# A feed-forward block on one core: a third Winograd pair, its products summed in two PSUM banks, and copies moved to ScalarE

## The chip, the cores and the metric

The kernel runs on one core of a Trainium2 chip. Four engines matter: TensorE (PE in the profile) multiplies, reading its operands from SBUF and adding its results up in PSUM, which has eight banks of 128 x 512 numbers; VectorE (DVE) and ScalarE (ACT) do elementwise work; GpSimd (POOL) does a little. Loads are issued from SyncE's queue (SP). Each engine works through its own queue in order and waits there for semaphores of the others. The metric is the device time of one execution in microseconds (us), smaller is better.

## The reference, cut to what matters

One block of a streaming encoder on 256 tokens of width 1024, in float32: a half-weighted feed-forward, a mixer of two branches (a gated linear recurrence, "HGRN", and a forgetting attention), a cross attention to a memory of 256 rows, and a second half-weighted feed-forward. Every stage has an RMS norm before and after.

```python
def swiglu(h, w_in, w_down):
    gate, up = jnp.split(h @ w_in, 2, axis=-1)
    return (jax.nn.silu(gate) * up) @ w_down

h = rmsnorm(x, ffn1_pre_g[l])
x = x + 0.5 * rmsnorm(swiglu(h, ffn1_w_in[l], ffn1_w_down[l]), ffn1_post_g[l])
...  # mixer, cross attention
h = rmsnorm(x, ffn2_pre_g[l])
x = x + 0.5 * rmsnorm(swiglu(h, ffn2_w_in[l], ffn2_w_down[l]), ffn2_post_g[l])
```

`w_in` is 1024 x 5632 and `w_down` 2816 x 1024 in each feed-forward.

## The kernel before

**Numbers in two parts.** Each float32 operand x is split in a rounded part `hi` (a cast, by ScalarE) and a remainder `lo` = x − hi (a subtraction, by VectorE). A product is then three matmuls, hi·hi + hi·lo + lo·hi. `load_split` does this for a weight tile of 128 x 1024 that SyncE has loaded into a `raw` buffer (lines 147 and 149), `split` for any other tile (lines 167 and 168). Buffers rotate: 4 `raw`, 8 `hi`, 8 `lo`, and 4 `extra` in which the tiles `sraw` of weights to be summed lie. A load waits until the tile that was in its buffer has been split or summed.

**Chunks of a feed-forward.** `ffn` works through 11 chunks (`NFF`) of 256 gate and 256 up columns of `w_in`; a chunk's weights are four tiles of 128 x 1024. There are four ways to make a chunk:

- *by tokens* (`act_tok`): for each half h of 128 tokens, 24 matmuls of 512 columns (gate and up beside each other) into one `mm` bank. `act_evac` then makes silu(gate) on ScalarE and its product with up on VectorE, and `flush` turns the result into columns with four transposes (line 438) into a `tr` bank, which is split.
- *by columns* (`act_col`): the weights are the stationary operand and the result is already transposed. Four blocks, each of 8 matmuls of 512 columns (weights' hi with both parts of x beside each other, class `Joined`), and 8 of 256 (weights' lo with the tokens' hi). `added` adds the two halves of the bank: a copy `plo` on ScalarE (line 219) and an addition on VectorE (line 221), four times a chunk.
- *first* (`act_first`): the chunks at the beginning, block by block of the inner dimension as the data arrive. Chunks 0, 1 and 2 of the first feed-forward are made so; the second makes its chunks 0 and 1 by tokens.
- *as a pair* (`act_pair(c, between)`): chunks c and c + 1 together, by Winograd's form of the 2 x 2 block product with seven block products instead of eight. The blocks of the left operand are two halves of the tokens by two halves of the inner dimension, those of the right operand two halves of the inner dimension by two chunks. Each of the seven `product`s is 12 matmuls of 512 columns. The left sums are made once in a feed-forward by `pair_inputs` (tiles `ss` and `sx`); it starts from `xf`, the input in float32, which in the first feed-forward `pair_joined` adds up out of hi and lo on VectorE (line 512). The right sums are made for each pair on VectorE (`add`, line 578), eight additions of 128 x 1024, on tiles that `sum_load` and `raws` have loaded. Seven products take 14 splits of 128 x 1024. The product p1 is needed twice, so it is copied out of its bank (`S.copy(p1, b0)`), as is p3; v, w and the outputs `c11`, `c01`, `c10` are combined by five VectorE operations of 128 x 512.

`PAIRS` and `TOKS` say how the later chunks are made; what is in neither is made by columns:

```python
TOKS = {"f1_in": (), "f2_in": (2, 5)}
PAIRS = {"f1_in": (6, 9), "f2_in": (3, 6, 9)}
```

So in the first feed-forward chunks 3, 4, 5 and 8 are made by columns, and (6, 7) and (9, 10) are pairs; in the second only chunk 8 is made by columns.

**Down projections.** `down(c, h)` multiplies a chunk's activations by two tiles of `w_down`, into four `acc` banks that add up all chunks. The kernel puts them between the chunks and, inside a pair, between the products: `between` is a list of halves of down projections and `step_between` issues the next one (12 matmuls of 512 columns). The last three chunks' down projections come at the end.

**PSUM.** 4 `acc` banks, 2 `mm`, 2 `tr`. A pair uses an `mm` bank for p1 and, added to it, the product with the raw block (b0); three `tr` allocations for b2, b3 and b1; and a second `mm` bank for b4, in which the products ad and e are added up one after the other.

**What sets the order.** The program's order is that of the code, moved by a scheduler that takes dependencies and priorities: work under `tc.high_priority()` goes ahead on its engine, `tc.issue_after(x)` holds it back until x, and `after(i)` places work behind the i-th matmul (`log`). On TensorE matmuls stand as they are issued; `flush(n)` places the transposes of a chunk 21 or so matmuls into later work. On VectorE and ScalarE splits, sums, combinations and evacuations are interleaved in the order in which the scheduler takes them to become ready.

**Start.** Eight `head` tiles hold a block of x (transposed), its gains and 512 columns of weights. For each, ScalarE casts the weights (line 785) and the gained x (`gain_split`, line 366; the first one's hi is made by VectorE), and VectorE makes both remainders.

**The HGRN stage.** The recurrence's score products are made in six sets (`SETS`), each at `after(r0 + R_AT[si])`, between the matmuls of the gates (`proj_tok` with 344 columns, line 1044) and of the attention's k and q. Between sets `grow` multiplies decays into K and Q on VectorE (lines 973 to 996), `gather` and `stash` copy parts out of them on ScalarE, and `keep` takes the products out of PSUM. `grow` overwrites the K and Q that the set before has read. The gates' `mm` banks are evacuated by ScalarE (line 1046) and VectorE (line 1047).

## Time and profile before

| | |
|---|---|
| median of three runs | 774.85 us (774.65 to 775.62) |
| profiled execution | 773.87 us, span 771.6 us |
| granted TensorE clock | 0.998 |
| TensorE busy | 763.9 us (99%) |
| VectorE busy | 647.0 us (84%) |
| ScalarE busy | 493.5 us (64%) |
| first feed-forward | about 5 to 173 us of the span |
| HGRN products' first three sets | about 258 to 288 us |

The profile comes from one execution. Its span runs from the first to the last instruction; the time of the execution is 2.3 us longer. In a timeline row stand the start, the busy time, the engine, the line of the code, the operation, what is written and read (buffer numbers left out), the shape and the count; in brackets the idle time of that engine just before and what ended it. Nearly all matmuls have line 97, that of the helper `MM`, so they are told apart by the tiles that they write and read. Matmuls are pipelined: the duration of one is longer than the distance to the next. A group row gives the count, then the busy time in us and the mean in ns, then idle time before the group's instructions. In a row of a window stand the start and end, its length, the busy time and count of TensorE, of its weight loads, of VectorE, of ScalarE and of GpSimd, the granted clock, the share of DMA time and the GB/s.

### The profile page before, as it was taken

Reading aid. Unit: us, or ns where it says so; the run is one execution under the profiler, and the core shown is the slowest. Engines: PE = TensorE matmul, PEld = TensorE weight load, DVE = VectorE, ACT = ScalarE, POOL = GpSimd, SP = SyncE. Lnnn points to the kernel's source line nnn. Section 1 sums busy time; section 2 is a strip of 40 time slices with the busy share of each in tenths; the row PEclk is TensorE's granted clock in tenths of the full one; section 3 lists DMA queues with packets and bytes.
Section 4 is the critical chain, followed back from the end, with each engine's and each line's share of the span. In section 5 each row is a group of like instructions: output and inputs, shape, how many; then the busy total and the mean of one; then the engine's idle time right before and its main releaser. Section 6 shows DMA issues by size and latency. Waiting matters only on the chain.

```text
span 771.6 us, 11832 instructions
## 1 busy us (share of the span) xinstructions
PE 763.9 (99%) x4398; PEld 650.3 (84%) x4398; DVE 647.0 (84%) x992; ACT 493.5 (64%) x803; POOL 17.2 (2%) x39
## 2 busy tenths in 40 slices
PE   9999999999999999999999999999999999999996
PEld 7888888888888998898888888889888888888885
DVE  7798998998778899988776665885679999999993
ACT  7666565768764678667676345862768567665762
POOL 0000000000000101200000000000000000000000
PEclk9999999999999999999999999999999999999999
DMA  9758386255744445834576654456075726467231
GB/s 339 267 197 290 120 287 248 93 203 196 226 164 147 168 155 186 307 108 158 199 264 234 216 169 161 165 186 223 24 247 186 259 110 216 167 231 287 82 138 55
DMA packets 44505, 148.06 MB, mean 192 GB/s; under 512 B 5144, under 2 KB 8864, under 8 KB 44448
## 3 DMA queue, kind: packets, MB, share of 16 engines
q1 hardware_dynamic: 43168, 144.83, 53.5%
q0 software_dynamic: 848, 2.12, 1.0%
q8 instruction: 34, 0.56, 0.3%
q10 hardware_dynamic: 432, 0.37, 0.1%
q14 instruction: 23, 0.19, 0.1%
HBM read 146.24 MB, written 1.06 MB: 191 GB/s over the span
## 4 chain that ended last, share of the span: by engine, by line
PE 98%; DMA 1%; DVE 0%; ACT 0%; issue 0%; SPq 0%; DVEq 0%; ACTq 0%
PE mm L97 45%; PE acc L97 39%; PE tr L97 12%; PE tr L438 1%; PE tr L379 1%; DMA head<-in_head_dram 1%; PE tr L1211 0%; PE tr L1305 0%; PE acc L1424 0%; DVE xs L415 0%; DVE post L410 0%; ACT hi L785 0%; ACT hlT L366 0%; SPq L769 0%; SPq L764 0%
## 5 line engine op out<-in xcount | busy, mean ns | idle before, releaser
L149 DVE TENSOR_TENSOR lo<-raw,hi 128x1024 fp32r<-128x1024 f32 (+1 forms) x212 | 251.4, 1202 | 37.5 <-ACT hi L147 30.9
L147 ACT CAST hi<-raw 128x1024 fp32r<-128x1024 f32 (+1 forms) x212 | 215.4, 1034 | 74.4 <-PE mm L97 35.0
L97 PE MATMUL mm<-hi,hlT 128*128 128x512 f32 (+1 forms) x624 | 190.2, 381 | 0.0
L97 PEld LDWEIGHTS mm<-hi,hlT 128*128 128x128 f32 x624 | 115.3, 188 | 19.7
L97 PE MATMUL mm<-lo,hlT 128*128 128x512 f32 (+1 forms) x312 | 117.5, 381 | 0.0
L97 PE MATMUL acc<-hi,act 128*128 128x512 f32 x352 | 113.4, 390 | 0.0
L97 PEld LDWEIGHTS acc<-hi,act 128*128 128x128 f32 x352 | 66.1, 188 | 13.7 <-ACT act L167 0.3
L167 ACT CAST hi<-sraw 128x1024 fp32r<-128x1024 f32 x50 | 52.0, 1054 | 27.3 <-DVE sraw L578 19.4
L97 PE MATMUL acc<-lo,act 128*128 128x512 f32 x176 | 69.4, 394 | 0.0
L97 PEld LDWEIGHTS mm<-lo,hlT 128*128 128x128 f32 x312 | 58.5, 188 | 9.7 <-DVE lo L149 0.2
L97 PE MATMUL acc<-hlT,hi 128*128 128x512 f32 x256 | 64.4, 393 | 0.0
L168 DVE TENSOR_TENSOR lo<-sraw,hi 128x1024 fp32r<-128x1024 f32 x50 | 60.2, 1218 | 0.0
L97 PEld LDWEIGHTS acc<-hlT,hi 128*128 128x128 f32 x256 | 46.1, 189 | 8.3
L97 PE MATMUL mm<-hlT,hi 128*128 128x512 f32 (+1 forms) x192 | 44.0, 357 | 0.0
L97 PE MATMUL tr<-hi,sx 128*128 128x512 f32 x120 | 39.3, 391 | 0.0
L97 PEld LDWEIGHTS acc<-lo,act 128*128 128x128 f32 x176 | 33.1, 188 | 7.2 <-DVE lo L149 0.7
L97 PEld LDWEIGHTS acc<-hlT,lo 128*128 128x128 f32 x256 | 35.0, 190 | 2.5
L97 PEld LDWEIGHTS mm<-hlT,hi 128*128 128x128 f32 x192 | 33.2, 189 | 4.4
L97 PE MATMUL acc<-hlT,lo 128*128 128x256 f32 x256 | 36.2, 283 | 0.0
L578 DVE TENSOR_TENSOR sraw<-sraw,raw 128x1024 f32<-128x1024 f32 x30 | 35.9, 1219 | 0.1
L97 PE MATMUL tr<-hlT,hi 128*128 128x512 f32 x128 | 32.6, 394 | 0.0
L97 PE MATMUL mm<-hlT,lo 128*128 128x256 f32 x160 | 27.7, 284 | 0.0
(293 smaller groups left out, 1277.1 us busy)
## 6 DMA issues: line engine op xcount, KB each, us to landing
raw<-in_wts_dram SPq DMA_DIRECT2D x227, 512.0 KB, 4.3
sraw<-in_wts_dram SPq DMA_DIRECT2D x20, 512.0 KB, 5.1
raw<-in_gf_dram SPq DMA_DIRECT2D x12, 344.0 KB, 3.8
head<-in_head_dram SPq DMA_DIRECT2D x7, 392.0 KB, 6.6
grow<-in_rows_dram SPq DMA_DIRECT2D x4, 512.0 KB, 5.4
xs<-in_x_dram SPq DMA_DIRECT2D x2, 512.0 KB, 7.8
cbm<-cd POOLq DMA_DIRECT2D x2, 512.0 KB, 6.4
brow<-in_rows_dram SPq DMA_DIRECT2D x4, 256.0 KB, 3.6
```

The lines of the kernel that those rows point to most:

```text
L97: log.append(PE.matmul(*args, **kw).ins)
L147: S.copy(h, r)
L149: V.tensor_tensor(out=l, in0=r, in1=h.bitcast(F32), op=ALU.subtract)
L167: a = S.copy(hi, src)
L168: b = V.tensor_tensor(out=lo, in0=src, in1=hi.bitcast(F32), op=ALU.subtract)
L379: PE.transpose(blocks[-1][1], src(kb), ident)
L438: PE.transpose(trv[:, j, h * P : (h + 1) * P], ats[c, h][:, j * P : (j + 1) * P], ident)
L578: V.tensor_tensor(out=x, in0=x, in1=y, op=ALU.add)
```

## The change

Six things change together.

1. `PAIRS["f1_in"]` gets a third pair, (4, 5), which stands directly before the pair (6, 7). Those chunks were made by columns.
2. `TOKS` gets chunks 3 and 8 in the first feed-forward and chunk 8 in the second. Those were made by columns.
3. `act_pair` adds its products up in two `mm` banks: b1 holds p1, then + aed, + ad, + e; b4 holds de, then + baed. Signs of the left sums and the roles of the two chunks are turned round so that each partial sum is a wanted term: after p1, after aed (v) and after ad (w), ScalarE copies b1 out; after de it copies b4 (p5). The product with the raw block, b0, has a `tr` bank of its own. VectorE combines three times instead of five (`c01` = b4 − v, `c11` = p5 − w, `c00` = p1 + b0); the fourth output is read from b1 directly. ScalarE copies four times instead of two.
4. The products come in the order p1, de, aed, baed, ad, b0, e (before: p1, baed, de, aed, b0, ad, e), and the right sums are made in that order, still eight additions a pair.
5. `xf` of the first feed-forward is made in the start by ScalarE, eight activations of 128 x 256 straight from the heads, instead of four VectorE additions of 128 x 512 in chunk 2.
6. The first three entries of `R_AT` go from 24, 126, 210 to 66, 130, 188.

```diff
@@ -33,9 +33,9 @@
 
 STAG = 3
 
-TOKS = {"f1_in": (), "f2_in": (2, 5)}
-
-PAIRS = {"f1_in": (6, 9), "f2_in": (3, 6, 9)}
+TOKS = {"f1_in": (3, 8), "f2_in": (2, 5, 8)}
+PAIRS = {"f1_in": (4, 6, 9), "f2_in": (3, 6, 9)}
 
 L_ACT = 21
 L_F1 = 24
@@ -53,7 +53,7 @@
 M_T = (106, 119)
 M_O = (136, 140)
 
-R_AT = (24, 126, 210, 252, 286, 318)
+R_AT = (66, 130, 188, 252, 286, 318)
 
 R_GROW = ((1, 0), (2, 1))
 
@@ -505,6 +505,8 @@
 
 
 
         def pair_joined(k):
             t = m4([P, 4, T], n="xf")
             for i in range(2):
@@ -525,11 +527,11 @@
             ss = [m4([P, 2, 4, P], n="ss") for _ in range(2)]
             de, aed, ad, baed = (t[:, i] for t in ss for i in range(2))
             V.tensor_tensor(out=de, in0=d, in1=e, op=ALU.subtract)
-            V.tensor_tensor(out=aed, in0=a, in1=de, op=ALU.subtract)
+            V.tensor_tensor(out=aed, in0=de, in1=a, op=ALU.subtract)
             V.tensor_tensor(out=ad, in0=a, in1=d, op=ALU.subtract)
-            V.tensor_tensor(out=baed, in0=b, in1=aed, op=ALU.subtract)
+            V.tensor_tensor(out=baed, in0=b, in1=aed, op=ALU.add)
             out = {}
-            for n, x in (("baed", baed), ("aed", aed), ("de", de), ("ad", ad), ("e", e)):
+            for n, x in (("de", de), ("aed", aed), ("baed", baed), ("ad", ad), ("e", e)):
                 t = m4([P, 2, 4, P], F32R, "sx")
                 split(t[:, 0], t[:, 1], x)
                 out[n] = t
@@ -544,7 +546,7 @@
             return t
 
         def more(r, c, k, n, j, op):
-            src = wts[_AT[w_in] + 4 * (c + n) + 2 * k + j - 4]
+            src = wts[_AT[w_in] + 4 * (c + 1 - n) + 2 * k + j - 4]
             if op is None:
                 loads.append(nc.sync.dma_start(r, src).ins)
             else:
@@ -592,52 +594,48 @@
                 return sp.tile([P, 512], F32, tag="z2", name=nm(n), bufs=3)
 
             sums, both = sums_of_pair.pop(c)
-            vw = m4([P, 2, 512], n="vw")
-            pc = m4([P, 2, 512], n="pc")
-            p1, p3, v, w = pc[:, 0], pc[:, 1], vw[:, 0], vw[:, 1]
-            b0 = mm()
-            product(b0, of_x(0), splits(sums), True)
-            S.copy(p1, b0)
+            copies = [m4([P, 2, 512], n=n) for n in ("vw", "pc")]
+            p1, v, w, p5 = (t[:, i] for t in copies for i in range(2))
+            b1 = mm()
+            product(b1, of_x(0), splits(sums), True)
+            S.copy(p1, b1)
+            add(sums, both)
             for _ in range(2 if c == 3 else 1):
                 step_between()
-            b2 = trp()
+            b4 = mm()
+            product(b4, of("de"), splits(sums), True)
+            S.copy(p5, b4)
+            step_between()
             raw = raws(1, 1)
-            product(b2, of("baed"), splits(raw), True)
-            S.copy(p3, b2)
+            add(sums, raw)
+            product(b1, of("aed"), splits(sums), False)
+            S.copy(v, b1)
             step_between()
-            add(sums, both)
+            product(b4, of("baed"), splits(raw), False)
             add(both, raw)
-            b3 = trp()
-            product(b3, of("de"), splits(sums), True)
-            add(sums, raw)
-            step_between()
-            b1 = trp()
-            product(b1, of("aed"), splits(sums), True)
             with tc.high_priority():
-                V.tensor_tensor(out=v, in0=p1, in1=b1, op=ALU.subtract)
-                V.tensor_tensor(out=w, in0=b3, in1=v, op=ALU.subtract)
-            step_between()
-            raw = raws(1, 0)
-            product(b0, of_x(1), splits(raw), False)
-            with tc.high_priority():
-                act_evac(b0, c, 0)
-            add(sums, raw)
-            step_between()
-            b4 = mm()
-            product(b4, of("ad"), splits(both), True)
+                t = half_tile("c01")
+                V.tensor_tensor(out=t, in0=b4, in1=v, op=ALU.subtract)
+                act_evac(t, c, 0)
+            product(b1, of("ad"), splits(both), False)
+            S.copy(w, b1)
             with tc.high_priority():
                 t = half_tile("c11")
-                V.tensor_tensor(out=t, in0=w, in1=b4, op=ALU.subtract)
-                act_evac(t, c + 1, 1, r2[0], q)
-                t = half_tile("c01")
-                V.tensor_tensor(out=t, in0=w, in1=p3, op=ALU.add)
+                V.tensor_tensor(out=t, in0=p5, in1=w, op=ALU.subtract)
+                act_evac(t, c, 1, r2[0], q)
+            step_between()
+            b0 = trp()
+            raw = raws(1, 0)
+            product(b0, of_x(1), splits(raw), True)
+            add(sums, raw)
+            with tc.high_priority():
+                t = half_tile("c00")
+                V.tensor_tensor(out=t, in0=p1, in1=b0, op=ALU.add)
                 act_evac(t, c + 1, 0)
             step_between()
-            product(b4, of("e"), splits(sums), False)
+            product(b1, of("e"), splits(sums), False)
             with tc.high_priority():
-                t = half_tile("c10")
-                V.tensor_tensor(out=t, in0=v, in1=b4, op=ALU.add)
-                silu = act_evac(t, c, 1, r2[0], q)
+                silu = act_evac(b1, c + 1, 1, r2[0], q)
             if c + 1 == NFF - 1:
                 table(silu)
             while between:
@@ -721,7 +719,7 @@
                 accs = [[acc(), acc()], [acc(), acc()]]
             if c == 2 and pairs:
                 if first_half:
-                    xf = [pair_joined(k) for k in range(2)]
+                    xf = xf1
                 pairs_in = pair_inputs()
 
             while done < (NFF - STAG if last == NFF - 1 else min(c - 1 - (c + 1 in pairs), NFF - STAG - 1)):
@@ -755,6 +753,7 @@
 
 
     X1 = Joined()
+    xf1 = [m4([P, 4, T], n="xf") for _ in range(2)]
     heads, raw1 = [], []
     for kb in range(KB):
         heads.append(wp.tile([P, D], F32, tag="extra" if kb in (1, 2, 3, 4, 6) else "raw", name=nm("head"), bufs=4))
@@ -785,6 +784,7 @@
                 S.copy(hi, w)
             if c == 0:
                 gain_split(X1, kb, heads[kb][:, :T], heads[kb][:, T + kb : T + kb + 1], first=kb == 0)
+                S.activation(xf1[kb // 4][:, kb % 4], heads[kb][:, :T], AF.Copy, scale=heads[kb][:, T + kb : T + kb + 1])
             lo_last = V.tensor_tensor(out=lo, in0=w, in1=hi.bitcast(F32), op=ALU.subtract).ins
 
     def norm_1():
```

## The prediction

> **What bounds the kernel now.** I read the page's first two parts and the chain that ended last, then what TensorE waited for.
>
> ```profile
> span 771.6 us, 11832 instructions
> PE 763.9 (99%) x4398; PEld 650.3 (84%) x4398; DVE 647.0 (84%) x992; ACT 493.5 (64%) x803; POOL 17.2 (2%) x39
> PE 98%; DMA 1%; DVE 0%; ACT 0%; issue 0%; SPq 0%; DVEq 0%; ACTq 0%
> ```
>
> ```profile
> PE tr L97 <- PEq L1563: 0.8, 1, 0.8
> PE acc L97 <- ACT hlT L366: 0.3, 1, 0.3
> ```
>
> TensorE is the bound and has almost no named wait, 1.1 us in all. So its own stream can only get shorter by holding less matmul time, and any other engine costs something only where it becomes late. "mean ns" of a matmul group is a pipelined duration; the price is the distance between starts, from the timeline of one chunk by columns (chunk 4) of the first feed-forward:
>
> ```profile
> 61.70 1.98 PE L97 MATMUL mm<-hlT,hi 128*128 128x512 f32 x8
> 63.51 1.12 PE L97 MATMUL mm<-hlT,lo 128*128 128x256 f32 x8
> 64.47 2.00 PE L97 MATMUL mm<-hlT,hi 128*128 128x512 f32 x8
> ...
> 72.85 0.40 PE L97 MATMUL acc<-hi,act 128*128 128x512 f32 x1
> ```
>
> Eight of 512 columns take 63.51 − 61.70 = 1.81 us, 0.227 each; eight of 256 take 64.47 − 63.51 = 0.96, 0.120 each; the chunk 72.85 − 61.70 = 11.15 us. [...] The measured spacing decides.
>
> VectorE is the next engine. Its load over the first feed-forward:
>
> ```profile
> 120.00:150.00 30.00, 30.00 (x153) 25.25 (x152) 29.52 (x35) 19.45 (x28) 0.00 (x0) 1.00 0.39 142
> 30.00:180.00 150.00, 150.00 (x734) 125.95 (x734) 139.66 (x167) 96.31 (x130) 0.00 (x0) 1.00 0.61 214
> 600.00:740.00 140.00, 140.00 (x647) 115.58 (x645) 135.89 (x160) 90.00 (x113) 1.17 (x2) 1.00 0.52 186
> ```
>
> After the stretch and its length come TensorE, its weight loads, VectorE and ScalarE. From 30 to 180 VectorE is busy for 139.7 of 150 us, so 10.3 idle; ScalarE, with 96.3, has room. In the second feed-forward, 600 to 740, VectorE has 4.1 idle. VectorE keeps up because it runs ahead; the next rows show by how much at the start of pair 6 and in pair 9.
>
> ```profile
> 74.99 1.22 DVE L168 TENSOR_TENSOR lo<-sraw,hi 128x1024 fp32r<-128x1024 f32 x1
> ...
> 158.48 1.22 DVE L149 TENSOR_TENSOR lo<-raw,hi 128x1024 fp32r<-128x1024 f32 x1
> ```
>
> ```profile
> 89.69 0.40 PE L97 MATMUL mm<-lo,hlT 128*128 128x512 f32 x1
> ...
> 159.75 0.50 PE L97 MATMUL acc<-lo,act 128*128 128x512 f32 x1
> ```
>
> Pair 6's first `lo` is ready at 76.2 and used at 89.69: 13.5 us ahead. The split that ends at 159.70 is used at 159.75: nothing ahead. A pair eats the lead, the chunks between restore it.
>
> **The change part by part: TensorE.** Chunks 4 and 5 by columns are 2 × 11.15 = 22.3 us. A pair is 7 products of 12 matmuls of 512 columns, 84 × 0.227 = 19.1, and 8 transposes of its activations. Those have this row:
>
> ```profile
> L438 PE MATMUL tr<-ident,at 128*128 128x128 f32 x68 | 10.3, 274 | 0.0
> ```
>
> 0.274 is the pipelined duration; the spacing lies between 0 and that, and 0.11 is in line with the 0.120 above: 0.9 us. A third pair saves 22.3 − 20.0 = 2.3 us. A chunk by tokens is 48 × 0.227 + 4 × 0.11 = 11.3, 0.2 more than by columns; chunks 3 and 8 of the first and 8 of the second feed-forward cost 0.6. Over the kernel that is 68 matmuls of 512 columns more (+15.4), 160 of 256 fewer (−19.2) and 20 transposes more (+2.2): **−1.6 us**, and −1.7 by the chunks. I take −1.6. Weight bytes and loads stay as many; a pair reads its raws in another order on SP's queue and never twice.
>
> **VectorE in the first feed-forward.** Its prices:
>
> ```profile
> L149 DVE TENSOR_TENSOR lo<-raw,hi 128x1024 fp32r<-128x1024 f32 x200 | 241.2, 1221 | 35.2 <-ACT hi L147 28.6 <-PE acc L97 2.7 <-PE tr L97 1.8
> L578 DVE TENSOR_TENSOR sraw<-sraw,raw 128x1024 f32<-128x1024 f32 x30 | 35.9, 1219 | 0.1
> L221 DVE TENSOR_TENSOR up<-tr,plo 128x256 f32<-128x256 f32 x10 | 4.2, 420 | 1.9 <-ACT plo L219 1.9
> L618 DVE TENSOR_TENSOR vw<-tr,vw 128x512 f32<-128x512 f32 x5 | 3.4, 683 | 0.0
> L512 DVE TENSOR_TENSOR xf<-hlT 128x512 f32<-128x512 f32 x8 | 5.3, 680 | 0.0
> ```
>
> Back to back each overlaps the next by about 0.08: 1.14 for 1024 columns, 0.34 for 256, 0.60 for 512. A pair holds 14 splits and 8 sums of weight tiles (22 × 1.14 = 25.1), three combinations of products (1.8; five before), four products with silu (1.6) and two activation splits (1.2): 29.7 us. By columns a chunk holds 4 splits, 4 additions and three or four of 512: 7.9 (11.15 on TensorE); by tokens 4 splits, two products and one split: 5.8. So the third pair adds 29.7 − 15.8 = 13.9, the two chunks by tokens give 4.2 back, the two combinations dropped from each old pair 2.4, xf 4 × 0.60 = 2.4: **+4.9 us of VectorE on 10.3 idle, while TensorE's time there shrinks by 1.9.** That leaves 3.5 us idle in about 148. Some of the idle time is not to be had: VectorE waits for ScalarE's `hi`, for loads or for TensorE to free a buffer.
>
> ```profile
> DVE lo L149 <- ACT hi L147: 4.9, 7, 2.1
> DVE up L221 <- ACT plo L219: 1.9, 2, 1.0
> DVE act L168 <- ACT act L167: 0.9, 2, 0.6
> DVE lo L168 <- PE tr L97: 0.8, 1, 0.8
> DVE lo L149 <- PE tr L97: 0.7, 1, 0.7
> ```
>
> Waits for `plo` go with the chunks by columns; those for `hi` (4.9) mostly stay, and they are above 3.5. What is short becomes a stall: between 0 (the waits shrink when VectorE is late) and 4.9 + 0.8 − 3.5 = 2.2, with one more us above for the place: pairs 4 and 6 stand back to back, with no chunk between that restores a lead. Summing VectorE's queue in its new order with these prices, its leads shrink by some 5 us through pairs 4 and 6 and at the end, and the early waits take most of what is left. I take **+0.8 (0 to 3)**. First to be late: the transposes of the last two activations of pair 4, the splits of pair 6's sums, whose four `extra` slots pair 4 frees only when its last sum is cast (a load of 5.1 us, next row, lies behind that), and the splits of `w_down` near the end of pair 9.
>
> ```profile
> sraw<-in_wts_dram SPq DMA_DIRECT2D x20, 512.0 KB, 5.1
> ```
>
> **ScalarE.** Per pair two copies more of a bank; xf adds eight activations at the start.
>
> ```profile
> L600 ACT COPY pc<-mm 128x512 f32<-128x512 f32 x5 | 2.9, 579 | 0.0
> L366 ACT ACTIVATE hlT<-head 128x256 fp32r<-128x256 f32 x7 | 3.5, 505 | 0.0
> L147 ACT CAST hi<-raw 128x1024 fp32r<-128x1024 f32 x200 | 206.9, 1051 | 74.4 <-PE mm L97 35.0 <-DMA raw<-in_wts_dram 29.8 <-PE acc L97 4.2
> ```
>
> The copies are 1.2 us a pair on an engine at 64%. But a product that adds to a bank now waits for the copy of what was in it. Behind the copies stand `hi` casts, 1.05 each; between a product and the next one in the same bank lies one other product or half a down projection, 12 × 0.227 = 2.7 us. One cast and the copy fit in that, 1.6 us; three queued casts would not. Price 0, up to 0.5 a pair. xf is 8 × 0.5 = 4 us; the first stands ahead of the first `hi` and delays the first matmul by 0.5.
>
> ```profile
> 6.99 0.61 PE L97 MATMUL acc<-lo,hlT 128*128 128x512 f32 x2
> 7.89 1.45 PE L97 MATMUL acc<-hi,hlT 128*128 128x512 f32 x4 [0.28 <-ACT hlT L366]
> 9.18 0.62 PE L97 MATMUL acc<-lo,hlT 128*128 128x512 f32 x2
> ```
>
> TensorE stands still there anyway for the next head: 7.89 − 6.99 − 0.45 = 0.44, and 9.18 − 7.89 − 0.91 = 0.38. So the 0.5 is covered; uncovered it costs 0.5. The later seven lie among ScalarE's casts, and ahead of the first silu stands idle time that takes them:
>
> ```profile
> 25.93 0.47 ACT L443 ACTIVATE sg<-acc,facs 128x256 f32<-128x256 f32 x1 [3.31 <-PE acc L97]
> ```
>
> Of 3.5 us, 3.3 fit: 0.
>
> **The second feed-forward.** Chunk 8 by tokens is in the sum. VectorE loses 2.1 and 3 × 1.2 there. Pair 3 now takes de second, and its `ss` and `sx` tiles are made in another order; before, the first sx was used as it was ready:
>
> ```profile
> 633.07 2.50 DVE L168 TENSOR_TENSOR sx<-ss,sx 128x512 fp32r<-128x512 f32 x4
> ```
>
> ```profile
> 633.14 0.44 PE L97 MATMUL tr<-hi,sx 128*128 128x512 f32 x1
> ```
>
> de comes 2.3 us earlier on TensorE, and its inputs, no longer behind three subtractions and an sx, some 2.9 earlier. I take **+0.1 (−0.3 to +1.0)**.
>
> **R_AT.** HGRN's first products go from 24 to 66 matmuls after the first gate matmul; the next growth of K and Q must wait for them. The second set stays where it was in time, the third comes 2.7 us earlier.
>
> ```profile
> 267.66 0.69 DVE L986 TENSOR_TENSOR k<-k,aux 128x512 f32<-128x512 f32 x1
> ...
> 272.04 0.58 DVE L1047 SCALAR_TENSOR_TENSOR G<-mm,facs,z 128x344 f32<-128x344 f32 x1
> ```
>
> ```profile
> 275.10 0.75 PE L97 MATMUL acc<-q,early 128*32 128x32 f32 x63
> ```
>
> The first growth (4 × 0.60) and four masked copies (1.2), now after the products' end at about 266, push the second growth (before at 267.66) to 269.6 and the evacuation `G` at 272.04 to about 274.5; the `mm` bank that it frees is wanted at 274.3, the products at 275.1 want its gathers, ready at 273.6. **+0.3 (0 to 1.2).** Before has no stall here to win back.
>
> **Sum.** −1.6 + 0.8 + 0.1 + 0.3 = −0.4 us against the profiled execution's 773.87: 773.5. The runs' median, 774.85, is 1.0 above the profiled one, so 774.4.
>
> **The rivals.** *Nothing becomes late.* VectorE's waits for `hi` come from running ahead and vanish when it does not; stalls are 0, and relief in the second feed-forward removes the few tenths at the splits with no lead. −1.6 − 0.2 = −1.8: 773.0. For it: the late waits in the list are all VectorE's own, and 3.5 us stay idle; against it: no lead is left at 159.75 already before.
>
> *VectorE becomes the bound in the pairs: slower.* A down projection between its products is 2 splits, 2.3 of VectorE, against 24 × 0.227 = 5.45 of TensorE. So pair 4 with three needs 29.7 + 6.9 = 36.6 against 20.0 + 16.3 = 36.3, pair 6 with two 34.3 against 30.9, pair 9 with one 32.0 against 25.4: short by 0.3, 3.4 and 6.6, of which chunk 8 gives 5.5 back. A split must be ready some 2 us ahead. With a lead L at the start of pair 4, pairs 4 and 6 stall for 3.7 + 2 − L, and pair 9 for 1.1 (near the 0.8 that I took). Before pair 6 of the old order L was 13.5, after three chunks by columns; before pair 4 stand one chunk by tokens and pair_inputs with five splits. The rival decides at L = 4: 1.7 + 1.1 = 2.8 of stall, +1.6 in all. At L = 2 it is 4.8, so −1.6 + 4.8 + 0.4 = +3.6, and 778.5 in the median. Against it: the sum of the queue has L at 7 or more.
>
> *Copies between products hold the bank.* Five restarts a pair that wait half a us, six pairs, would be +10; the slots of 2.7 us speak against all of them, some in pair 3, where five sx casts stand ahead of p1's copy, may show. [...]
>
> **How the numbers follow.** 0.2% or 1.55 us is what a measurement tells from no change: faster is below 773.3, slower above 776.4. The forecast, 774.4 with its own range 773.3 to 776.0, has 0.42; nothing late 0.33; VectorE the bound 0.20; copies 0.05. Range: from −2.4 (nothing late, with −0.3 in the second feed-forward and some idle won at the start), 772.4, to the bounds 3, 1.0 and 1.2 partly together, 777.8.
>
> **What would show it.** The end of the first feed-forward about 1 us earlier than before. From pair 4 to pair 9: waits of TensorE on `at`, `lo` or `act` in 75 to 165 of 0 to 3 us in sum; VectorE above 14.5 of each 15 us there. `PE mm <- ACT vw` or `pc` would show the bank rival; a wait near 274 for `G`, R_AT. Wrong it would be if VectorE's lead before pair 4 is below 4 us, or if waits turn up that the order alone does not show.

## The result and the profile after

The changed kernel takes 777.98 us in the median of six runs (776.60 to 779.58), the kernel before 774.58 in the runs beside them: a ratio of 1.0045, 95% interval 1.003 to 1.006. It is slower by 3.4 us, 0.2 us above the upper end of the range. The profiled execution is the longest of the six, 779.58 us, so its losses are a little larger than those of the median: its span is 5.7 us longer than before's.

The first parts of its page, and the chain that ended last:

```profile
span 777.3 us, 11682 instructions
PE 765.9 (99%) x4326; PEld 648.1 (83%) x4326; DVE 647.3 (83%) x975; ACT 504.2 (65%) x816; POOL 17.5 (2%) x39
PE 79%; DVE 11%; ACT 4%; DMA 3%; issue 2%; SPq 0%; DVEq 0%; ACTq 0%
```

TensorE has 72 instructions fewer and still is busy for 2 us longer. The chain is the line to look at: 98% of it was TensorE before, now a fifth runs over VectorE, ScalarE and loads. What TensorE waited for, in us in total, number of times and longest:

```profile
PE mm L97 <- DVE lo L149: 2.0, 1, 2.0
PE tr L97 <- PEq L1563: 0.8, 1, 0.8
PE acc L97 <- DVE lo L149: 0.6, 2, 0.3
PE mm L97 <- ACT hi L167: 0.5, 1, 0.5
PE mm L97 <- ACT sx L167: 0.4, 1, 0.4
```

One wait of 2.0 us stands out, and it is in none of the places that the prediction named. To see the small losses too, I summed over each stage what the distance between two matmul starts exceeds the spacing of its form (0.227, 0.120, 0.158 and 0.109 us for 512, 256, 344 and 128 columns). That counts waits, slow matmuls and a lowered clock alike; the tiny HGRN products are not in it.

| beyond the spacing, us | start, 0 to 20 | first feed-forward and behind, 20 to 200 | HGRN stage, 240 to 360 | second feed-forward, from 600 | all |
|---|---|---|---|---|---|
| before | 2.6 | 0.8 | 1.4 | 1.0 | 8.5 |
| changed | 3.3 | 3.5 | 5.3 | 1.1 | 15.9 |
| changed, `R_AT` 60 (below) | 2.4 | 3.3 | 1.4 | 1.2 | 11.2 |

The difference, 7.4, less the 1.6 of matmul time saved, is 5.8; the span says 5.7. So the saving is there, and 3.9 of the loss is in the HGRN stage, 2.6 (3.46 − 0.84) around the first feed-forward. The HGRN stage first: VectorE and TensorE between 306 and 312 us.

```profile
306.13 1.22 DVE L149 TENSOR_TENSOR lo<-raw,hi 128x1024 fp32r<-128x1024 f32 x1
307.26 0.68 DVE L986 TENSOR_TENSOR k<-k,tq 128x512 f32<-128x512 f32 x1
...
309.67 0.68 DVE L986 TENSOR_TENSOR qf<-qf,tq 128x512 f32<-128x512 f32 x1
310.27 0.42 DVE L221 TENSOR_TENSOR q_b<-mm,plo 128x256 f32<-128x256 f32 x1
310.61 1.22 DVE L149 TENSOR_TENSOR lo<-raw,hi 128x1024 fp32r<-128x1024 f32 x1
```

```profile
308.99 0.87 PE L97 MATMUL mm<-hlT,lo 128*128 128x256 f32 x6
311.88 0.39 PE L97 MATMUL mm<-hlT,lo 128*128 128x256 f32 x1 [2.02 <-DVE lo L149]
```

The `lo` that TensorE wants at 309.8 stands in VectorE's queue behind the growth of K and Q for the sixth set (line 986, four of them, with a `kp` split between), and is ready at 311.8. In the kernel before it stands ahead of them, as the second of the two in the first row:

```profile
302.88 2.35 DVE L149 TENSOR_TENSOR lo<-raw,hi 128x1024 fp32r<-128x1024 f32 x2
...
305.16 0.68 DVE L986 TENSOR_TENSOR k<-k,tq 128x512 f32<-128x512 f32 x1
```

Behind the wait TensorE's clock is lowered. In windows of the changed kernel the third number from the right is the granted clock:

```profile
308.00:312.00 4.00, 1.99 (x13) 1.58 (x12) 4.00 (x7) 1.32 (x2) 0.66 (x1) 1.00 0.94 247
312.00:316.00 4.00, 4.00 (x21) 3.81 (x22) 4.00 (x6) 2.45 (x5) 0.97 (x2) 0.60 0.85 275
316.00:320.00 4.00, 4.00 (x22) 3.45 (x21) 2.98 (x6) 1.41 (x3) 0.14 (x1) 0.97 0.91 293
30.00:180.00 150.00, 148.88 (x675) 121.86 (x674) 143.37 (x157) 101.82 (x131) 0.00 (x0) 1.00 0.61 211
```

0.60 over 4 us and 0.97 over the next 4 are 1.7 us lost beside the 2.0. The trace has the clock at 0.50 for 3.41 us, from 312.82 on; the last section sets this gap beside others. The last row is the first feed-forward: VectorE is busy for 143.4 of 150 us (139.7 before), and TensorE no longer without a gap.

In the first feed-forward the waits are short and spread. Where pair 4 begins, on TensorE, and on ScalarE and VectorE:

```profile
57.38 0.47 PE L97 MATMUL mm<-hi,hlT 128*128 128x512 f32 x1 [0.52 <-ACT hi L167]
57.68 0.40 PE L97 MATMUL mm<-lo,hlT 128*128 128x512 f32 x1
```

```profile
55.36 1.99 ACT L167 CAST hi<-sraw 128x1024 fp32r<-128x1024 f32 x2
```

```profile
44.91 1.16 DVE L168 TENSOR_TENSOR lo<-sraw,hi 128x1024 fp32r<-128x1024 f32 x1
46.18 1.22 DVE L168 TENSOR_TENSOR lo<-sraw,hi 128x1024 fp32r<-128x1024 f32 x1
...
53.20 2.50 DVE L168 TENSOR_TENSOR sx<-ss,sx 128x512 fp32r<-128x512 f32 x4
...
56.81 0.42 DVE L446 TENSOR_TENSOR at<-mm,sg 128x256 f32<-128x256 f32 x1
...
59.74 2.36 DVE L168 TENSOR_TENSOR lo<-sraw,hi 128x1024 fp32r<-128x1024 f32 x2
```

The profile puts the wait of 0.52 us down to a cast, but those two casts (55.36) are of the pair's second product: their `lo` come from 59.74 on, while the first product uses its own `lo`, ready since 47.4, at 57.68. What TensorE waits for is VectorE. Directly ahead of the matmul TensorE's queue waits for VectorE's semaphore until 57.24, and the operation that ends then is the `at` at 56.81. It takes the first half of chunk 3 out of the `mm` bank that the pair's first product needs. Its silu was ready at 52.58; on VectorE it stands behind the last left sum and six splits. At the end of pair 9 it is the splits of `w_down`:

```profile
170.26 0.51 PE L97 MATMUL acc<-lo,act 128*128 128x512 f32 x1 [0.30 <-DVE lo L149]
...
171.99 0.50 PE L97 MATMUL acc<-lo,act 128*128 128x512 f32 x1 [0.30 <-DVE lo L149]
```

```profile
166.64 1.05 ACT L147 CAST hi<-raw 128x1024 fp32r<-128x1024 f32 x1 [1.12 <-DMA raw<-in_wts_dram]
```

These splits are late because their tiles come late: ScalarE waited 1.12 us for the load of the first one. That load was issued at 161.58, when a split of VectorE that ended at 161.53 had freed its `raw` buffer, and landed at 166.56. So the time at which VectorE frees a buffer comes back by way of a load and a cast, and VectorE itself is idle for 1.5 us meanwhile.

### The profile page after: what moved, and what is told of

Same layout as the page of the kernel before. It is cut to its first block, busy times and chain, and to the rows that moved or that the text cites. A ratio compares the mean times of both kernels' runs of the same rounds, so it can differ in the third digit from the quotient of the medians.

```text
span 777.3 us, 11682 instructions
## 1 busy us (share of the span) xinstructions
PE 765.9 (99%) x4326; PEld 648.1 (83%) x4326; DVE 647.3 (83%) x975; ACT 504.2 (65%) x816; POOL 17.5 (2%) x39
## 4 chain that ended last, share of the span: by engine, by line
PE 79%; DVE 11%; ACT 4%; DMA 3%; issue 2%; SPq 0%; DVEq 0%; ACTq 0%
PE mm L97 39%; PE acc L97 33%; PE tr L97 4%; DVE lo L149 3%; DMA raw<-in_wts_dram 2%; DVE sraw L580 2%; ACT hi L147 1%; DVE lo L168 1%; DVE qf L986 1%; PE tr L438 1%; PE tr L379 1%; DVE k L986 1%; DMA head<-in_head_dram 1%; ACT hi L167 1%; ACT f L1024 0%
## 5 line engine op out<-in xcount | busy, mean ns | idle before, releaser
L97 PE MATMUL mm<-hi,hlT 128*128 128x512 f32 (+1 forms) x688 | 209.4, 382 | 0.5 <-ACT hi L167 0.5
L97 PEld LDWEIGHTS mm<-hi,hlT 128*128 128x128 f32 x688 | 127.2, 188 | 23.2 <-ACT hi L167 0.9
L97 PE MATMUL mm<-lo,hlT 128*128 128x512 f32 (+1 forms) x344 | 130.2, 382 | 0.1
L167 ACT CAST hi<-sraw 128x1024 fp32r<-128x1024 f32 x60 | 62.7, 1052 | 30.9 <-DVE sraw L580 23.6
L97 PE MATMUL mm<-hi,sx 128*128 128x512 f32 x240 | 77.7, 390 | 0.4 <-ACT sx L167 0.4
L168 DVE TENSOR_TENSOR lo<-sraw,hi 128x1024 fp32r<-128x1024 f32 x60 | 71.8, 1219 | 1.0 <-ACT hi L167 0.7
L97 PEld LDWEIGHTS mm<-hi,sx 128*128 128x128 f32 x240 | 45.0, 188 | 10.4 <-ACT sx L167 0.9
L97 PEld LDWEIGHTS acc<-hlT,hi 128*128 128x128 f32 x256 | 46.1, 189 | 8.3
L97 PE MATMUL mm<-lo,sx 128*128 128x512 f32 x120 | 46.7, 389 | 0.0
L168 DVE TENSOR_TENSOR lo<-raw,hi 128x1024 fp32r<-128x1024 f32 x24 | 28.5, 1220 | 0.0
L167 ACT CAST hi<-raw 128x1024 fp32r<-128x1024 f32 x24 | 24.6, 1049 | 3.5 <-DMA raw<-in_wts_dram 3.2
```

Of the source, the lines that this page charges most:

```text
L97: log.append(PE.matmul(*args, **kw).ins)
L167: a = S.copy(hi, src)
L168: b = V.tensor_tensor(out=lo, in0=src, in1=hi.bitcast(F32), op=ALU.subtract)
```

## The experiments

Each was timed against runs of the kernel before on the same chip; a ratio below is to those, with its 95% interval.

### Which part loses: R_AT or the pairs

`R_AT` alone in the kernel before:

```diff
-R_AT = (24, 126, 210, 252, 286, 318)
+R_AT = (66, 130, 188, 252, 286, 318)
```

> The kernel before with only R_AT's three entries changed. Theory A (the profile of the changed kernel: its longest wait, 2.0 us of a q_b matmul for a lo split near 310 us, comes from R_AT, which moves that split behind four growth steps of K and Q in VectorE's queue): a wait of 1 to 2 us at about 308 us, a dip of the granted clock behind it, and 2 to 4 us more than before. Theory B (the rival of the prediction: VectorE becomes the bound in the pairs of the first feed-forward, and the loss is there): within 0.5 us of before.

782.71 us, ratio 1.0109 (1.0096 to 1.0122): 8.3 us slower, more than the whole change costs. The wait for the `lo` is there, 2.0 us. But ahead of it is a longer one that neither theory had, in the first set of products:

```profile
PE acc L97 <- issue: 3.9, 1, 3.9
PE mm L97 <- DVE lo L149: 2.4, 2, 2.0
```

"issue" means that TensorE waited for no semaphore that the profile shows. Theory B falls, and A is not the whole.

The changed kernel with the old `R_AT` (the same diff, reversed, in the changed kernel):

> The changed kernel with the old R_AT. Theory A: the wait near 310 us goes, 2 to 4 us less than the changed kernel, so 774 to 776, within 1.5 us of before; what stays above the -1.6 us of saved matmul time is 0.7 in the start and 2 to 3 us around the first feed-forward. Theory B: about 3 us above before still.

778.45 us, ratio 1.0054 (1.0039 to 1.0068): as slow as the changed kernel. The wait for the `lo` is gone, as A says, but the new kind of wait has come in its place, in the same set of products, and the clock is lowered behind it (a window of 259 to 265 us has 0.72):

```profile
257.24 0.43 PE L97 MATMUL acc<-qf,early 128*32 128x32 f32 x28
259.59 0.48 PE L97 MATMUL acc<-qf,early 128*32 128x32 f32 x34 [1.92 <-issue]
```

xf added up by VectorE again, in the changed kernel:

```diff
-                S.activation(xf1[kb // 4][:, kb % 4], heads[kb][:, :T], AF.Copy, scale=heads[kb][:, T + kb : T + kb + 1])
...
-                    xf = xf1
+                    xf = [pair_joined(k) for k in range(2)]
```

> The changed kernel with xf added up by VectorE again, as before. Theory A: the first matmul comes 0.55 us earlier again, at 4.6 us; VectorE has 2.4 us more to do ahead of pair 4, so the waits of the first feed-forward grow by 0 to 2.4 us; -0.7 to +1.7 us against the changed kernel. Theory B: VectorE decides, so +2.4 us less the 0.7: +1.7.

780.53 us, ratio 1.0072 (1.006 to 1.0084), 2.1 us above the changed kernel by the ratios, 2.6 by the medians, a little above the upper end of 1.7; the two intervals leave some 1.5 us either way. Its waits for `lo` in down projections rise from 0.6 to 1.7 us, and the sum beyond the spacing around the first feed-forward from 3.5 to 6.5. The work put back is 2.4 us. So at that place VectorE's work comes out at the end about one for one: theory B's arithmetic holds for the first feed-forward, though not for the loss.

Without the third pair, in the changed kernel:

```diff
-PAIRS = {"f1_in": (4, 6, 9), "f2_in": (3, 6, 9)}
+PAIRS = {"f1_in": (6, 9), "f2_in": (3, 6, 9)}
```

> The changed kernel with only the pairs (6, 7) and (9, 10) in the first feed-forward, chunks 4 and 5 by columns again. Theory A: 2.3 us of matmul time come back, and of the waits of about 2.6 us around the first feed-forward some 1 to 2.6 us go; -0.5 to +1.5 us against the changed kernel, with the wait near 310 us unchanged. Theory B: the loss of 3.4 us goes with the third pair: 774 to 775.

779.28 us, ratio 1.0058 (1.0045 to 1.0071). The loss does not go with the pair, against B. It has the wait for the `lo` (2.0 us) and one of 1.5 us "issue", now just behind the first set of products:

```profile
270.68 0.43 PE L97 MATMUL mm<-hi,hlT 128*128 128x344 f32 x1 [1.50 <-issue]
```

### What the "issue" waits are

The three stand at fixed places of TensorE's program. Counting matmuls in the order of their starts, they come behind number 1499 (`R_AT` alone), 1371 (old `R_AT` in the changed kernel) and 1500 (two pairs): 128 apart, or at the same number to one record. The DMA part of the page of the kernel before has a number close to 128, with packets, MB and share:

```profile
q8 instruction: 34, 0.56, 0.3%
```

34 packets for 4398 matmuls, each with a weight load, are 16 KB and about 129 matmuls a packet, and in the trace of the kernel before the packets start 127.7 matmuls apart on the average (107 to 152 outside the first three HGRN sets). So I read a packet as a piece of TensorE's program of 128 matmuls, and the places of the three waits as ends of such pieces, at 1371 and 1499. The first HGRN set is 192 matmuls that take only 1.3 us in all for the 126 of one row; the starts of these 126 lie within 1.10 to 1.26 us, so a piece made of them is used up in about 1.2 us. From the end of one piece to the first instruction behind the next one it took 5.2, 3.4 and 5.6 us in the three; in the kernel before 6.5 us pass between the same two ends, and there is no wait. So the theory, C: TensorE stands still where one end falls into that set and the next one into it or close behind it.

| kernel | first set, numbers | ends in or just behind it | wait, us |
|---|---|---|---|
| before | 1274 to 1465 | 1371 (1499 is 34 behind) | none |
| changed | 1256 to 1447 | 1371 (1499 is 52 behind) | none |
| `R_AT` alone | 1316 to 1507 | 1371, 1499 | 3.9 |
| changed, old `R_AT` | 1214 to 1405 | 1243, 1371 | 1.9 |
| changed, two pairs | 1292 to 1483 | 1371, 1499 (16 behind) | 1.5 |
| changed, `R_AT` 60 (below) | 1250 to 1441 | 1371 (1243 is 7 ahead, 1499 is 58 behind) | none |
| before, `R_AT` 60 (below) | 1310 to 1501 | 1371, 1499 | 3.6 |

The trace also has the start and the duration of each packet of that queue, so the theory can be looked at directly. Windows cut around one packet show it: in the kernel before with `R_AT` 60 (below) no packet of the queue starts from 250 to 265.9 us, and one from 265.9 to 266.1:

```profile
q8 instruction: 1, 0.02, 28.3%
```

| kernel | an end is passed (us) | the next packet starts | it has landed | the next end's matmuls are wanted | TensorE goes on |
|---|---|---|---|---|---|
| `R_AT` alone | 265.15 | 267.90 | 269.03 | 266.5 | 270.32 |
| changed, old `R_AT` | 256.19 | 257.26 | 258.21 | 257.7 | 259.59 |
| changed, two pairs | 265.12 | 268.24 | 269.14 | 269.2 | 270.68 |
| before, `R_AT` 60 | 263.53 | 266.00 | 266.91 | 264.8 | 268.49 |
| before | 257.82 | 258.90 | 260.05 | 264.27 | no wait |
| changed | 266.00 | 268.07 | 268.95 | 275.10 | no wait |
| changed, `R_AT` 60 | 262.01 | 259.98 | 260.93 | 264.12 | no wait |

In the seven rows the packet starts between 2.0 us before and 3.1 us after the end is passed; that it brings the matmuls behind the next end is my reading of these times. All four waits end 1.3 to 1.6 us behind the landing of the packet. The distance between two ends alone does not decide: in the last row they are 2.1 us apart without a wait, as they are in five further runs (2.1 to 2.3 us). There the first end lies among the gates' matmuls ahead of the set, and the packet starts 1.6 to 2.4 us before it; where the first end lies within the set, the packet starts 1.1 to 3.1 us behind it in the rows of the table. Why the start varies so is not shown.

The changed kernel has 60 matmuls fewer ahead of the set, so the same `R_AT` meets other ends. Two runs test this. First the changed kernel with an entry that avoids both troubles:

```diff
-R_AT = (66, 130, 188, 252, 286, 318)
+R_AT = (60, 126, 210, 252, 286, 318)
```

> The changed kernel with R_AT 60, 126, 210 in place of 66, 130, 188. Theory C, formed on the first four runs: two things in the HGRN stage cost time on TensorE. First, with 66 the last lo split of a q_b weight comes behind four growth steps in VectorE's queue (2.2 us near 310 us). Second, TensorE's instructions come in pieces of 16 KB, 128 matmuls with their weight loads, and the 256 tiny products of the first set use up a piece in 1.3 us; where a piece ends 60 to 190 products into the set, TensorE waits 2 to 4 us for the next. With 60 the split stands ahead of the growth again, and the pieces end at the 132nd product and behind the last: no wait of the first kind, none of the second above 1 us, the clock stays; 3 to 4 us less than the changed kernel's profile, a median of 774 to 775.5. Theory A (R_AT's order of VectorE alone): the same here, so this run does not part them, but a wait inside the first products would speak for C. Theory B (pairs): no gain.

774.78 us, ratio 0.9999 (0.9991 to 1.0008). (The set has 192 products, not the 256 of the expectation, and the end at 1371 falls on its 122nd.) No wait in the products, none at 310, clock 0.998; TensorE's sum in the HGRN stage is 1.4 us as before. `R_AT` is the whole measured loss. Second, the same entry in the kernel before, where it should do harm:

```diff
-R_AT = (24, 126, 210, 252, 286, 318)
+R_AT = (60, 126, 210, 252, 286, 318)
```

> The kernel before with R_AT's first entry 60 in place of 24 and nothing else. VectorE's order near 308 us is that of before. Theory C (instruction pieces of 128 matmuls, whose ends the earlier runs put at the 1371st and the 1499th matmul): the first HGRN set, 192 matmuls, begins at about the 1309th, so both ends fall into it, 1.2 us apart, and a new piece took 3.4 to 5.6 us from the end of the one before. So TensorE stands still for 2 to 4 us behind the 1499th matmul with no semaphore awaited, the clock is at half for some 3 to 7 us behind that, and the kernel is 4 to 7 us slower than before. If only VectorE's order was at fault in the run with R_AT alone: within 0.5 us of before.

781.41 us, ratio 1.0091 (1.0078 to 1.0105): 6.8 us slower, by one number that costs nothing in the changed kernel. The wait comes behind the 1499th matmul, two before the end of the set. Its timeline, and two windows:

```profile
264.12 0.72 PE L97 MATMUL acc<-qf,early 128*32 128x32 f32 x60
268.49 0.27 PE L97 MATMUL acc<-qf,early 128*32 128x32 f32 x2 [3.64 <-issue]
```

```profile
260.00:270.00 10.00, 6.36 (x217) 5.96 (x215) 6.13 (x11) 4.20 (x7) 1.66 (x8) 0.86 0.64 226
270.00:280.00 10.00, 10.00 (x53) 10.00 (x53) 7.90 (x17) 6.20 (x9) 1.04 (x5) 0.79 0.12 42
```

3.6 us of waiting, and 1.4 + 2.1 us by the clock (0.86 and 0.79 of 10 us each) are 7.1. No wait for a `lo` is in this run, so the two mechanisms are parted: VectorE's order gives 2 us plus the clock, the instructions 1.5 to 3.9, plus the clock behind all but the shortest (two pairs: 1.00 from 268 to 276 us).

### What the rest of the change is worth

With `R_AT` 60, the first piece of xf moved from ScalarE back to VectorE:

```diff
+                if kb:
                     S.activation(xf1[kb // 4][:, kb % 4], ...)
+                else:
+                    V.tensor_tensor(out=xf1[0][:, 0], in0=X1.hi(0).bitcast(F32), in1=X1.lo(0).bitcast(F32), op=ALU.add)
```

> As the run with R_AT 60, and the first of the eight xf pieces added by VectorE, so that ScalarE's first work is again the first hi cast. If the first xf activation delays the start: first matmul at 4.6 us in place of 5.15, and 0.5 us less than with R_AT 60 alone. If the start is paced by the heads' loads: no change within 0.2.

775.11 us, ratio 0.9999 (0.9991 to 1.0008): nothing. Over all profiles the start's sum lies between 2.2 and 3.3 us, with xf on ScalarE or not. The 0.7 us that the changed kernel's profile shows there belongs to that execution.

The pairs moved, with `R_AT` 60. First to the pattern of the second feed-forward:

```diff
-TOKS = {"f1_in": (3, 8), "f2_in": (2, 5, 8)}
-PAIRS = {"f1_in": (4, 6, 9), "f2_in": (3, 6, 9)}
+TOKS = {"f1_in": (5, 8), "f2_in": (2, 5, 8)}
+PAIRS = {"f1_in": (3, 6, 9), "f2_in": (3, 6, 9)}
```

> As the run with R_AT 60, but the first feed-forward in the pattern of the second: pairs (3, 4), (6, 7), (9, 10), with chunks 5 and 8 by tokens between them, so that no two pairs stand back to back. If the back-to-back pairs leave VectorE late (theory B): the waits in the first feed-forward, 0.7 near 56 us, 0.9 near 170 and 1.0 behind it up to 195, shrink to under 1 in all, 1 to 1.5 us less. If they come from the sum of VectorE's work, which is the same: within 0.5, or more where pair 3 starts before VectorE has its inputs.

780.63 us, ratio 1.0075 (1.0062 to 1.0087). The waits grow, first of all in the pair that now begins one chunk earlier (2.9 us for two `hi` casts, until 58 and 60 us; the first of the casts could start only when VectorE had ended its sum, at 56.8), then for transposes and activations near 130 and 177 us (1.2 and 0.9). Then, from the version with xf's first piece on VectorE, pairs (4, 5), (7, 8), (9, 10) and chunks 3 and 6 by tokens:

> As the run with R_AT 60 and the first xf by VectorE, but pairs (4, 5), (7, 8), (9, 10) and chunks 3 and 6 by tokens. If pairs back to back are what makes VectorE late, the waits move to the end of the first feed-forward, where nothing restores the lead, and grow: +1 to +3 us. If the waits are local to what stands in the queues, about the same, within 1.

776.54 us, ratio 1.0029 (1.0018 to 1.0041), against 0.9999 of the others with `R_AT` 60; one wait of 2.2 us, until 161.2, for the `hi` cast of a `w_down` tile inside pair 9 makes most of it. On ScalarE that cast stands behind one that started at 159.12, as VectorE's sum for it ended at 159.05. The size, 2.3 us by the ratios, is that of the expectation's first branch, with the wait in the second of two pairs back to back. But the pattern of the second feed-forward has no pairs back to back and is slower still. So the place chosen in the change is the best of the three tried; what the waits looked at have in common is an operation that stands behind late sums or splits of VectorE. A rule for the place does not follow from three runs.

The new `act_pair` and `pair_inputs` alone in the kernel before (chunks, pairs, xf and `R_AT` as before):

> The kernel before with only the new act_pair and pair_inputs: the same chunks, pairs, xf and R_AT as before, the products in two banks and in the new order. Theory C: no loss of note in the first feed-forward, 0.5 us at pair 3 of the second, where the sx casts of de come late on ScalarE: 0 to +0.7 us against before. The bank rival of the prediction: a wait at each restart, +2 us or more.

777.15 us, ratio 1.0028 (1.0017 to 1.0038): 2.1 us slower, above my 0 to 0.7. Not one of its waits is for a copy, so the bank rival's mechanism is not there; they are at the ends of pairs, for the last activations:

```profile
PE acc L97 <- DVE act L168: 1.3, 2, 0.7
PE tr L438 <- DVE at L448: 1.0, 2, 0.8
```

Tokens and xf alone in the kernel before (pairs, `act_pair` and `R_AT` as before):

> The kernel before with chunks 3 and 8 of the first and 8 of the second feed-forward by tokens and xf by ScalarE; pairs, act_pair and R_AT as before. Matmul time +0.6; VectorE has 6.6 us less to do in the first feed-forward; the first matmul comes up to 0.55 us later. +0.3 us, between -0.5 and +1.2.

775.56 us, ratio 1.0013 (1.0004 to 1.0022): 1.0 slower, against 0.6 of added matmul time. And both together, which is the changed kernel without the third pair and with the old `R_AT`:

> The changed kernel with the old R_AT and without the third pair: tokens, xf by ScalarE and the two banks stay. If the two banks cost 2.1 us by themselves, as the run with them alone says, and the relief of VectorE does not reach the ends of the pairs: +2 to +2.5 us against before, and the third pair is then worth -2 to -2.5, all of its matmul time. If the relief of VectorE takes those waits away: +0 to +1, and the third pair is worth under 1 us.

774.14 us, ratio 0.9995 (0.9986 to 1.0004). Alone the parts cost 2.1 and 1.0 us, together nothing. In its first feed-forward the sum beyond the spacing is 1.2 us, against 3.4 with the two banks alone, and VectorE is busy for 132.1 of 150 us:

```profile
30.00:180.00 150.00, 149.74 (x707) 124.45 (x706) 132.10 (x152) 96.86 (x128) 0.00 (x0) 1.00 0.62 219
```

That VectorE's relief is what takes the waits away is argued from this, not shown by a run of its own. The third pair, added to this (the version with `R_AT` 60), leaves the ratio where it is, 0.9999: it saves 2.3 us of matmul time, and the sum around the first feed-forward rises from 1.2 to 3.3 us. None of the kernels is faster than before beyond its interval.

## Why the prediction was wrong, step by step

**The saved matmul time** (−1.6 us) was right: the span follows from it and the sums to 0.1 us.

**R_AT is the step that failed** ("+0.3, 0 to 1.2", and "Before has no stall here to win back"). It measured 3.6 us (ratios 1.0045 and 0.9999 with `R_AT` 60) and 3.9 in the profile. That is against an entry without stalls. Against the old entry it costs nothing in the changed kernel (1.0045 and 1.0054), because that entry, harmless before, meets two ends of pieces there; in the kernel before the same edit costs 8.3 us. So the step had two faults: it missed the stalls, and it took the price of an entry as something that can be added to the other parts of the change. The prediction followed the work that moves with the entry to the nearest deadlines, at 274 and 275 us, and those held: TensorE has no gap there in the changed kernel. It left out three things. The entry also changes what the scheduler puts where 45 us later, and there one split fell behind five operations and a sum (2.0 us); that is in the order of the instructions, which could be read beforehand. Behind the gap of 2.0 us the clock stood at 0.50 for 3.41 us (1.7 us). And the position of the tiny products against the pieces of TensorE's program was never considered; the change happens to avoid that one, so it does not enter its own loss, but four other runs waited 1.5 to 3.9 us there.

**The stalls of the first feed-forward** ("+0.8, 0 to 3"): the mechanism was right, VectorE with too little idle time, and the size was off. The sum rose from 0.8 to 3.5 in the changed kernel (2.6 more, within the range but three times the 0.8), and with `R_AT` 60 2.1 of it comes with the third pair (1.2 to 3.3), which takes nearly its whole gain. Of the three places named, one held, the splits of `w_down` at the end of pair 9. The transposes of pair 4 and the sums of pair 6 were on time. The loss at the beginning of pair 4 was not named: the prediction measured VectorE's lead by the splits, and pair 4's first `lo` was 11.6 us ahead (ready at 46.1, used at 57.7), well above the 7 that it argued for. But the `at` that frees the bank had no lead, because it stood behind the left sums and their splits. The busy time from 75 to 165 us came out as worked out (14.6 to 15.0 of each 15 us on VectorE). From 30 to 180 VectorE still had 6.6 us idle, in place of the 3.5 worked out: its waits for ScalarE's `hi` fell by only 0.3 us (`lo` from 4.9 to 3.9, but `w` from 0.7 to 1.4).

**ScalarE's copies and xf** ("price 0"): no wait that the profiles put down to a copy out of a bank in any of the runs, and the start is unchanged within its scatter, so both stand. That the two banks alone cost 2.1 us at the ends of the pairs was not foreseen; the prediction counted only what they take off VectorE, and did not look at how late the last output now is.

**The second feed-forward** ("+0.1"): 0.1 by the sums. A wait for de's sx, 0.4 us near 636, is new, and the rest of the sum is smaller by about as much.

**The rivals.** "Nothing becomes late" is out. "VectorE becomes the bound in the pairs" is not the cause of the loss: the time comes back with `R_AT` alone and not with the third pair. But its arithmetic, one for one, is what moving xf showed. That the time came out near the 778.5 that it gave for a lead of 2 us is chance: the lead was 11.6. "Copies hold the bank" is out. The side on which the result lies had a chance of 0.25, for reasons that were not those at work.

## What to carry to other kernels

Where a scheduler sets the order, an edit of one position has to be followed through the whole order of every engine, not only to the next deadline: compare the queues before and after for each operation that something waits for. Here TensorE waited for 1.5 to 3.9 us in or just behind a burst of tiny matmuls (126 starts in 1.10 to 1.26 us) in four kernels and not in others, by the burst's position in the count of matmuls; so that position is a parameter of its own, and any edit that adds or removes matmuls ahead of it shifts it. A best value found for one version is then not a value for the next: 60 cost 6.8 us in one kernel and nothing in the other. And a lead is that of one operation: at pair 4 VectorE was 11.6 us ahead with the first split and 0.5 us late with the operation that frees the bank. Where the profile puts a wait down to an engine, check that what it names is an operand of what waited.

## What was not expected of the hardware

The queue that the page calls `instruction` moved 34 packets of 16 KB in the kernel before, one for about 129 matmuls with their weight loads. In four kernels TensorE stood still for 1.5 to 3.9 us in or just behind a burst of tiny matmuls, 126 of which start within 1.10 to 1.26 us, and went on 1.3 to 1.6 us after a packet of that queue had landed. With `R_AT` 60 in the changed kernel the packet had started 2.0 us ahead of the first of two ends of pieces 2.1 us apart, and there was no wait.

The clock stood at 0.50 for 3.41 us behind gaps of 1.9 and 2.0 us in three traces and for 6.83 us behind gaps of 3.6 and 3.9 us in two; behind three gaps of 2.0 to 2.2 us (two pairs, near 312; `R_AT` alone, near 317; the last pattern of pairs, near 160) it stayed at 1.00. The traces show with what this went. In the changed kernel's the stretches of one clock are 307.200 us at 1.00, 3.413 at 0.50 and 457.386 at 1.00, that is 90, 1 and 134 times 3.4133 us; the 764.585 us at 1.00 in the kernel before are 224 times that. So I divided the traces into windows of that length, counted from a change of the clock. TensorE's busy time in such windows, with the granted clock as the third number from the right; the first two rows are of the changed kernel, the next two of the run with two pairs, the last two of `R_AT` alone:

```profile
309.41:312.82 3.41, 1.40 (x12) 1.19 (x12) 3.41 (x8) 1.31 (x2) 0.00 (x0) 1.00 0.92 263
312.82:316.23 3.41, 3.41 (x15) 3.22 (x15) 3.41 (x5) 2.68 (x5) 1.11 (x2) 0.50 0.85 285
311.14:314.55 3.41, 1.54 (x13) 1.54 (x14) 3.41 (x7) 1.50 (x3) 0.00 (x0) 1.00 1.01 298
314.55:317.96 3.41, 3.41 (x24) 3.07 (x23) 3.39 (x5) 2.61 (x5) 1.11 (x2) 1.00 0.84 273
314.04:317.45 3.41, 2.17 (x13) 1.73 (x11) 3.41 (x7) 1.37 (x3) 1.00 (x2) 1.00 0.90 235
317.45:320.86 3.41, 2.61 (x21) 2.52 (x22) 3.41 (x6) 1.93 (x3) 0.56 (x1) 1.00 0.94 311
```

Windows at full clock with 1.40 us busy (changed kernel) and 1.49 us (old `R_AT` in it) are followed by one at 0.50, those with 1.54 us (two pairs) and 2.17 us (`R_AT` alone) by one at 1.00. The gap of 2.0 us in the changed kernel fell into one window; in the two other runs of the table it fell across two. A first window at 0.50 with 2.2 us busy (`R_AT` 60 in the kernel before) and one with 2.8 us (`R_AT` alone) were followed by another at 0.50, the one of the changed kernel, busy throughout, by one at 1.00. This is read from the traces; no run moved a gap on purpose, and what sets the clock is not shown.

The windows lie differently in the three traces of the table: counted in steps of 3.4133 us from the start of the span, they begin 2.2, 0.5 and 0.0 us behind a step. So I estimate that the same gap can cost 1.7 us more in one execution than in another, half of 3.41 us; each kernel has one trace, so no run shows it. That may be part of why the changed kernel's runs scatter over 3.0 us and those of before, beside them, over 1.5; it was not tested, and the mean granted clocks of the six do not follow their times closely (778.34 us at 0.998, 777.45 at 0.995).
